# The entry of the FFN: the last ends of the sub-layer are recorded ahead of the ordinary products

## The chip, the cores and the metric

The kernel runs on one core of one Trainium2 chip. Its engines are TensorE (PE in the rows: matrix products and transposes), VectorE (DVE), ScalarE (ACT), GpSimd (POOL), and SyncE (SP), which issues most DMAs. The metric is the device time of one launch in microseconds.

## The reference, cut to what matters

One inference step of a decoder trunk of two layers, for 1024 prompt tokens and 32 sample tokens, all in float32. Layer 0 has a pooling and state-space mixer, layer 1 an attention. Each layer ends with an FFN between two norms, and it is the passage from the sub-layer into that FFN that is changed:

```python
hp = hp + rms_norm(y_p, g[1])
hp = hp + rms_norm(swiglu_ffn(rms_norm(hp, g[2]), ffn_w_gate[layer], ffn_w_up[layer], ffn_w_down[layer]), g[3])

def swiglu_ffn(x, w_gate, w_up, w_down):
    return (jax.nn.silu(x @ w_gate) * (x @ w_up)) @ w_down
```

`y_p` is the output projection of the mixer, `x @ w_out`, of 1024 columns; the hidden width of the FFN is 2816. The sample tokens take the same path (`hs`, `y_s`).

## The kernel before

**Numbers in two parts.** Every float32 operand of a product is split into a high part (`whi` for weights, cast on ScalarE) and a low part (`wlo`, a subtraction on GpSimd or VectorE). A product is then three matmuls, lines 171 to 173 (`mm3`): high by high, low by high, high by low.

**The tokens.** The 1056 tokens are kept in columns, in four quarters (0 to 3); the output projection (`proj_out`) makes quarters 0 and 2 first, then 1, then 3. Each quarter ends in tiles of 128 tokens: tiles 6 and 7 are those of quarter 3, and tile 8 holds the 32 sample tokens. Tiles 6, 8 and 7, in this order, are the last ends of the sub-layer.

**The end of a tile** (`Boundary`, driven by the three-stage pipeline `Tiles`) is this chain. Eight transposes turn the tile into token rows in a PSUM bank (`turn`, line 329, bank `tp`, of which there are two). ScalarE squares and sums it (line 207) and takes the root (line 209). VectorE takes the reciprocal (211), scales (338) and adds the residual (342); the residual's rows `h` are loaded by SP (line 419 or 411) into one of two buffers. The same norm is made once more of the sum (`stats2`), with the normed rows `xs` (line 353, one buffer), and eight transposes turn them back (`turn2`, line 360). `Blocks` then writes them, split in two parts, as the operand blocks of the FFN: for the first half of the tokens `left` alone (B11, B21: lines 265 and 266), for the second half also `right1`, `right2` and `right3` (lines 279 to 296), which make B22 and the sums T1 to T4 in a scratch buffer `tmp` that exists once.

**The FFN's products.** Gate and up products are made for chunks of 256 hidden columns. Each chunk uses seven block products instead of eight (`seven`, bank `pp`), with sums S1 to S4 of the weights (`Weights.split`, lines 1151 to 1165: casts on ScalarE, low parts on GpSimd, sums on VectorE). For chunk 0, the quarters 0 and 2 (pair 0) are multiplied by ordinary products (`plain`, bank `mm`, 96 matmuls for gate and 96 for up), which need only B11, B21, B12 and B22 of that pair; these are ready before the last three ends. The gate product goes through Silu into `ct` (line 1256), and the up product is multiplied into it (`put0`, line 1252) and stored to `hd`. Quarters 1 and 3 of chunk 0, and all of the other ten chunks, go through `seven`.

**What sets the order.** In this part no order is written out. The recorded instructions go to a scheduler, which keeps one list for each engine; among the instructions that are ready in its own model of time, the one recorded earlier goes first. `proj_out` is a generator: it yields `po, ct` before its last three tiles, and the loop over `poc` records them. Each engine then runs its list strictly in order. Weights come through two shared buffers `wraw`, which free up when ScalarE and GpSimd have read them; `raws(kind)` with a kind takes a buffer of the scope `xS` instead, here `xe`, which T4 of pair 1 uses later. S1 to S4 lie where B12 lay, so they wait for the last ordinary product that reads B12.

Of the kernel before, what the change touches and what calls it, by code (L numbers as in the profile page):

```python
# [12 lines left out]
AF = mybir.ActivationFunctionType  # L13
# [41 lines left out]
def dram_ap(base, offset, pattern):  # L55
    return bass.AP(tensor=base.tensor, offset=base.offset + offset, ap=[list(x) for x in pattern])
# [3 lines left out]
def step_kernel(ctx, tc, x_prompt, x_sample, state_pool, state_s5, cache_k, cache_v, norm_gains,  # L60
# [6 lines left out]
    V, A, G, T = nc.vector, nc.scalar, nc.gpsimd, nc.tensor  # L67
# [29 lines left out]
    def nm(s):  # L97
        uid[0] += 1
        return f"{s}_{uid[0]}"

    def mmbank():
        return banks[-1].pool.tile([P, 512], F32, name=nm("mm"), tag="mm", bufs=banks[-1].mm)
# [67 lines left out]
    def mm3(ps, wh, wl, xh, xl, start, stop):  # L170
        T.matmul(ps, wh, xh, start=start, stop=False)  # L171
        T.matmul(ps, wl, xh, start=False, stop=False)  # L172
        T.matmul(ps, wh, xl, start=False, stop=stop)  # L173
# [864 lines left out]
    for j in range(2):  # L1038
        pt = mmbank()
        T.transpose(pt[:, 0:P], h0[:, j * P:(j + 1) * P], ident)  # L1040
        o = s5.tile([P, 64, 2], F32, name=nm("s5o"), tag="ut", bufs=4)
# [10 lines left out]
    with tc.tile_pool(name="glu", bufs=2) as glu:  # L1052
        wg = [weights(dram_ap(w_glu, j * 256, [[512, P], [P * 512, 4], [1, 256]]), a=4) for j in range(2)]
        for y in yS.q:
# [4 lines left out]
            for m in range(4):  # L1059
                wh, wl = wg[m // 2]  # L1060
                ms = slice((m % 2) * P, (m % 2) * P + P)
                ps = mmbank()
# [65 lines left out]
    def ffn(layer, xS, Y, poc, after, side):  # L1128
# [88 lines left out]
        def raws(kind):  # L1217
            if kind:
                t = xS.pool.tile([P, 2, 4, 256], F32, name=nm("raw2"), tag=kind, bufs=1)
                return [t[:, h] for h in range(2)]  # L1220
            return [wraw().rearrange("p (k c) -> p k c", k=4) for _ in range(2)]
# [6 lines left out]
        def plain(w, kind, evac):  # L1228

            rs = raws(kind)  # L1230
            ws = []
            for j, raw in enumerate(rs):
                nc.sync.dma_start(raw, dram_ap(w, base + j * 512 * HID, [[HID, P], [P * HID, 4], [1, 256]]))
                hi, lo = (wpool.tile([P, 1024], F32R, name=nm(n), tag=n, bufs=4).rearrange("p (k i c) -> p k i c", k=4, i=2)
                          for n in ("whi", "wlo"))
                A.copy(hi, four(raw))
                G.tensor_tensor(lo, four(raw), hi.bitcast(F32), op=sub)
                ws.append((hi, lo))
            ps = [mmbank() for _ in range(2)]
            for j, names in ((1, ("B12", "B22")), (0, ("B11", "B21"))):  # L1240
                for i in range(2):
                    for half, name in enumerate(names):
                        bh, bl = blk[name, 0]
                        wh, wl = ws[half]
                        for k in range(4):
                            mm3(ps[i][:, j * 256:j * 256 + 256], wh[:, k, i], wl[:, k, i], bh[:, k], bl[:, k],
                                half == 0 and k == 0, half == 1 and k == 3)
            for i in range(2):
                evac(i, ps[i], ct[:, 4 * (w is w_up) + 2 * i:4 * (w is w_up) + 2 * i + 2].rearrange("p a b -> p (a b)"))
# [3 lines left out]
            for j in range(2):  # L1253
                nc.scalar.dma_start(hd[i][:, j * HALF:j * HALF + 256], o[:, j * 256:j * 256 + 256])

        plain(w_gate, None, lambda i, ps, o: A.activation(o, ps, AF.Silu))
        plain(w_up, "xe", put0)
        for _ in poc:
            pass
        po.close()  # L1260
        f = Scope(nm("ffn"), side)
        banks[-1].close()
# [77 lines left out]
    def after0():  # L1340
# [10 lines left out]
        return done  # L1351

    ffn(0, x1S, yS, poc, after0, "left")
    norm_scope.pop().close()
    x2S = nxt["x"]
# [37 lines left out]
    class Project:  # L1393
# [27 lines left out]
        def evac(self, n0, n, ps):  # L1421
            a, c = n0 // P, (min(n0 + n, SEQ) - n0) // P
            nat = lambda t: t[:, :SEQ].rearrange("p (c s) -> p s c", s=L)[:, a:a + c]
            src = ps[:, 0:c * P].rearrange("p (s c) -> p s c", s=c)
            if self.part == 0:
                A.activation(nat(self.hi), src, AF.Copy, scale=0.125)
                V.scalar_tensor_tensor(nat(self.lo), src, 0.125, nat(self.hi).bitcast(F32), op0=mult, op1=sub)
            else:
                A.copy(nat(self.ft), src)
            if n0 + n == NT:  # L1430
                rows = ps[:, c * P:n].rearrange("p (t b) -> p t b", t=TS)
                if self.part == 0:
                    A.activation(self.rows, ps[:, c * P:n], AF.Copy, scale=0.125)
                else:
                    A.copy(self.rows.rearrange("p (b t) -> p t b", t=TS), rows)
# [618 lines left out]
    def after1():  # L2054
# [10 lines left out]
        return done  # L2065

    ffn(1, x3S, y1S, poc, after1, "right")
    norm_scope.pop().close()
    banks[-1].close()
# [46 lines left out]
```

## Time and profile before

| | |
|---|---|
| median of 3 runs | 2817.33 us (2815.06 to 2820.85) |
| the profiled execution | 2814.3 us, of which 2812.5 us are its span |
| TensorE busy | 2624.1 us, 93% |
| VectorE, GpSimd, ScalarE busy | 1666.5 us, 1380.5 us, 1112.8 us |
| FFN entry of layer 0 | products up to 444.74 us, last ends up to 477.46 us |
| FFN entry of layer 1 | products up to 2054.45 us, last ends up to 2087.13 us |

Times in the rows count from the start of the span. A timeline row gives start and length in microseconds, engine, line, operation, out<-in by the program's names, shape and count; in brackets stands how long the engine was idle before it, and what ended that. Rows of matmuls follow each other more closely than their lengths, since they are pipelined. A row of stretches gives the length, for each engine the busy time with the number of instructions, then the clock that TensorE was granted, as a share of full speed, the share of the DMA engines, and GB/s.

### The profile page before, as it was taken

What the parts mean: (1) busy time and instruction counts of PE and PEld (TensorE: products, weight loads), DVE (VectorE), ACT (ScalarE), POOL (GpSimd) and SP (SyncE); (2) the same over time, 40 slices, a digit from 0 to 9 for tenths busy, and PEclk for the clock granted to TensorE, in tenths of its full rate; (3) what the DMA queues carried; (4) which work ended last, traced back from release to release, by engine and by line L of the source; (5) the groups of instructions that cost most, each with busy time, mean ns of one, the idle gap of its engine ahead of it and who ended that gap; (6) DMA issues with size and microseconds to landing.
All of it is one profiled execution on the core that took longest, in us unless ns stands there. A gap on an engine that the chain in (4) does not pass through costs nothing.

```text
span 2812.5 us, 49713 instructions
## 1 busy us (share of the span) xinstructions
PE 2624.1 (93%) x19556; PEld 2527.7 (90%) x19556; DVE 1666.5 (59%) x3027; ACT 1112.8 (40%) x2033; POOL 1380.5 (49%) x1004
## 2 busy tenths in 40 slices
PE   6598996999999999989999999999969999999998
PEld 6587996999999999989899777778969999999998
DVE  8778375655554355743343699993766555543555
ACT  4134464222222311333344688884642222233112
POOL 4954454454554644012554466674543545455440
PEclk9799997999999999999999999999979999999999
DMA  5253452222122422243887666654622222232223
GB/s 150 101 194 117 121 188 79 84 81 84 65 92 83 154 92 92 86 159 124 230 251 205 167 170 159 165 144 143 197 77 75 86 73 83 74 107 93 92 92 131
DMA packets 272397, 348.64 MB, mean 124 GB/s; under 512 B 43864, under 2 KB 204380, under 8 KB 272156
## 3 DMA queue, kind: packets, MB, share of 16 engines
q1 hardware_dynamic: 213140, 287.72, 34.2%
q10 hardware_dynamic: 57872, 53.55, 5.6%
q0 software_dynamic: 1152, 4.19, 0.4%
q8 instruction: 154, 2.52, 0.4%
q14 instruction: 79, 0.65, 0.1%
HBM read 266.19 MB, written 79.39 MB: 123 GB/s over the span
## 4 chain that ended last, share of the span: by engine, by line
PE 74%; DVE 10%; DMA 5%; issue 4%; ACT 3%; POOL 2%; SPq 1%; ACTq 0%; POOLq 0%; DVEq 0%
PE pp L172 10%; PE pp L171 10%; PE pp L173 10%; PE mm L171 7%; PE mm L173 7%; PE mm L172 7%; PE tp L173 2%; PE tp L171 2%; PE tp L172 2%; PE tq L171 2%; PE tq L172 2%; PE tq L173 2%; PE pt L1910 1%; DVE pl L1927 1%; DVE Pr L1886 1%
## 5 line engine op out<-in xcount | busy, mean ns | idle before, releaser
L171 PE MATMUL pp<-blk,whi 128*128 128x272 f32 (+1 forms) x2352 | 673.6, 288 | 16.4 <-ACT blk L295 10.9
L172 PE MATMUL pp<-blk,wlo 128*128 128x272 f32 (+1 forms) x2352 | 676.3, 289 | 0.9 <-POOL wlo L1152 0.8
L173 PE MATMUL pp<-blk,whi 128*128 128x272 f32 (+1 forms) x2352 | 673.2, 287 | 0.0
L142 POOL TENSOR_TENSOR wlo<-wraw,whi 128x1024 fp32r<-128x1024 f32 x102 | 246.1, 2422 | 563.6 <-ACT whi L141 512.5
L171 PEld LDWEIGHTS pp<-blk,whi 128*128 128x128 f32 x2352 | 450.2, 192 | 17.4 <-ACT blk L295 11.5
L172 PEld LDWEIGHTS pp<-blk,wlo 128*128 128x128 f32 x2352 | 449.8, 192 | 1.4 <-POOL wlo L1152 1.4
L173 PEld LDWEIGHTS pp<-blk,whi 128*128 128x128 f32 x2352 | 450.2, 192 | 0.0
L1183 DVE TENSOR_TENSOR c<-pp,c 128x528 f32<-128x528 f32 (+1 forms) x308 | 209.2, 680 | 357.1 <-PE pp L173 351.0
L1152 POOL TENSOR_TENSOR wlo<-S,whi 128x1024 fp32r<-128x1024 f32 x82 | 199.5, 2433 | 371.9 <-ACT whi L1151 371.7
L141 ACT CAST whi<-wraw 128x1024 fp32r<-128x1024 f32 x126 | 131.1, 1053 | 357.7 <-PE mm L173 105.1
L1151 ACT CAST whi<-S 128x1024 fp32r<-128x1024 f32 x88 | 92.4, 1050 | 356.4 <-PE pp L173 332.8
L173 PE MATMUL mm<-hid,whi 128*128 128x256 f32 (+1 forms) x680 | 194.4, 286 | 8.1 <-POOL hid L1291 8.1
L171 PE MATMUL mm<-hid,whi 128*128 128x256 f32 (+1 forms) x680 | 197.6, 291 | 1.8 <-DVE yacc L1312 1.8
L172 PE MATMUL mm<-hid,wlo 128*128 128x256 f32 (+1 forms) x680 | 194.4, 286 | 0.0
L171 PE MATMUL mm<-y,whi 128*128 128x256 f32 (+1 forms) x576 | 167.4, 291 | 1.7 <-DVE s5o L1042 1.3
L172 PE MATMUL mm<-y,wlo 128*128 128x256 f32 (+1 forms) x576 | 166.9, 290 | 0.0
L173 PE MATMUL mm<-y,whi 128*128 128x256 f32 (+1 forms) x576 | 166.9, 290 | 0.0
L1312 DVE TENSOR_TENSOR yacc<-mm,yacc 128x272 f32<-128x272 f32 (+1 forms) x264 | 113.2, 431 | 81.5 <-PE mm L173 81.4
L171 PE MATMUL tp<-hid,whi 128*128 128x272 f32 x484 | 138.3, 286 | 0.0
L172 PE MATMUL tp<-hid,wlo 128*128 128x272 f32 x484 | 138.0, 285 | 0.0
L173 PE MATMUL tp<-hid,whi 128*128 128x272 f32 x484 | 137.7, 285 | 0.0
L173 PEld LDWEIGHTS mm<-hid,whi 128*128 128x128 f32 x680 | 128.7, 190 | 8.9 <-POOL hid L1291 8.9
(532 smaller groups left out, 7432.5 us busy)
## 6 DMA issues: line engine op xcount, KB each, us to landing
raw<-in_ffn_w_up_dram SPq DMA_DIRECT2D x48, 512.0 KB
wraw<-in_ffn_w_gate_dram SPq DMA_DIRECT2D x48, 512.0 KB
hid<-hd SPq DMA_DIRECT2D x44, 528.0 KB
wraw<-in_ffn_w_down_dram SPq DMA_DIRECT2D x44, 512.0 KB
hd<-c ACTq DMA_DIRECT2D x80, 264.0 KB
wraw<-in_ab_w_out_dram SPq DMA_DIRECT2D x24, 512.0 KB
wraw<-in_c_w_qkv_dram ACTq DMA_DIRECT2D x24, 512.0 KB
kt<-in_cache_k_dram SPq DMA_DIRECT2D x32, 384.0 KB
```

Of the source, the lines that this page charges most:

```text
L141: A.copy(hi[:rows], raw[:rows])
L142: lo_eng.tensor_tensor(lo[:rows], raw[:rows], hi[:rows].bitcast(F32), op=sub)
L171: T.matmul(ps, wh, xh, start=start, stop=False)
L172: T.matmul(ps, wl, xh, start=False, stop=False)
L173: T.matmul(ps, wh, xl, start=False, stop=stop)
L1151: A.copy(hi, src)
L1152: (V if early and src is S34 else G).tensor_tensor(lo, src, hi.bitcast(F32), op=sub)
L1183: plus = lambda o, ps, x: V.tensor_tensor(o, ps, x, op=add)
L1312: V.tensor_tensor(yo, ps[:, :n], yo, op=add)
L1886: V.tensor_tensor_reduce(out=self.p[:, c0:c0 + n], in0=ps, in1=strip[:, off:off + n], scale=-1.0, scalar=self.mx if part else -NEG, op0=ad ...
L1910: T.transpose(pt[:, j, r * P:(r + 1) * P], self.u.rows[r].p[:, (self.j0 + j) * P:(self.j0 + j + 1) * P], ident)
L1927: V.tensor_tensor(self.pl[:, a, b], self.pt[:, a, b], self.ph[:, a, b].bitcast(F32), op=sub)
```

## The change

The loop that records the last three tiles' ends moves ahead of the two ordinary products, so the scheduler prefers the ends where both are ready. The up product's raw weights lose their own buffer, since T4 has `xe` by then, and come through the two `wraw` buffers.

```diff
--- before.py
+++ after.py
@@ -1253,10 +1253,10 @@
             for j in range(2):
                 nc.scalar.dma_start(hd[i][:, j * HALF:j * HALF + 256], o[:, j * 256:j * 256 + 256])
 
-        plain(w_gate, None, lambda i, ps, o: A.activation(o, ps, AF.Silu))
-        plain(w_up, "xe", put0)
         for _ in poc:
             pass
+        plain(w_gate, None, lambda i, ps, o: A.activation(o, ps, AF.Silu))
+        plain(w_up, None, put0)
         po.close()
         f = Scope(nm("ffn"), side)
         banks[-1].close()
```

Each instruction of the ends, of the products and of chunk 0's weights is there before and after, apart from table loads of ScalarE. Their places in the lists differ, in both layers alike; beyond the entries only a few neighbours have changed places. Numbers in the names count the program's tiles and differ between the two programs.

**TensorE, layer 0, end of the ordinary products, before.** `mm_4565` is the second half of the up product, `tp` are the turns of tiles 6, 8 and 7 (from `yo`) and their second transposes (from `xs`), `pp` is the first block product:

```order
L171 MATMUL mm_4565<-blk_3715,whi_4560 128x256
L172 MATMUL mm_4565<-blk_3715,wlo_4561 128x256
L173 MATMUL mm_4565<-blk_3715,whi_4560 128x256
L329 MATMUL tp_4668<-ident,yo_4183 128x128 x8
L329 MATMUL tp_4686<-ident,yo_3843 32x128 x8
L329 MATMUL tp_4719<-ident,yo_4183 128x128 x8
L360 MATMUL tp_4730<-ident,xs_4717 128x128 x8
L360 MATMUL tp_4780<-ident,xs_4767 128x32 x8
L360 MATMUL tp_4821<-ident,xs_4811 128x128 x8
L171 MATMUL pp_4916<-blk_4160,whi_4863 128x272
```

**TensorE now, in the middle of the gate product.** `tp_4172` is the second transposes of tile 3, `mm_4634` the first half of the gate product, `tp_4441` the turn of tile 6:

```order
L360 MATMUL tp_4172<-ident,xs_4170 128x128 x8
L172 MATMUL mm_4634<-blk_3715,wlo_4626 128x256
L173 MATMUL mm_4634<-blk_3715,whi_4625 128x256
L171 MATMUL mm_4634<-blk_3715,whi_4625 128x256
L329 MATMUL tp_4441<-ident,yo_4183 128x128 x8
```

**TensorE now, end of the up product** (`mm_4747`):

```order
L171 MATMUL mm_4747<-blk_3715,whi_4742 128x256
L172 MATMUL mm_4747<-blk_3715,wlo_4743 128x256
L173 MATMUL mm_4747<-blk_3715,whi_4742 128x256
L360 MATMUL tp_4553<-ident,xs_4540 128x32 x8
L360 MATMUL tp_4594<-ident,xs_4584 128x128 x8
L171 MATMUL pp_4917<-blk_4160,whi_4864 128x272
```

The turn of tile 6 stands behind 55 of the 192 product matmuls, that of tile 8 behind 86, that of tile 7 behind 106, and the second transposes of tile 6 behind 151. Only the second transposes of tiles 8 and 7 are left behind the last product.

**ScalarE, layer 0, before.** `tp_4172` is tile 3, `tp_4668` tile 6, `tp_4686` tile 8, `mm_4453` and `mm_4454` the gate product, `whi` the first chunk's weights:

```order
L265 CAST blk_4160<-tp_4172 128x2x4x128
L1256 ACT_TABLE_LOAD
L1256 ACTIVATE ct_3166<-mm_4453 128x512
L1151 CAST whi_4863<-wraw_4857 128x4x128
L1256 ACTIVATE ct_3166<-mm_4454 128x512
L1151 CAST whi_4869<-S_800_4861 128x1024
L1254 DMA hd_4440<-ct_3166 128x256 x2
L1151 CAST whi_4873<-wraw_4858 128x1024
L1151 CAST whi_4879<-S_801_4862 128x1024
L1254 DMA hd_4440<-ct_3166 128x256 x2
L207 ACTIVATE junk_4679,ss_4680<-tp_4668 128x1024
L209 ACT_TABLE_LOAD
```

**ScalarE now, from tile 3 on.** `tp_4441` and `h_4450` are tile 6, `tp_4459` is tile 8, `mm_4634` and `mm_4635` the gate product:

```order
L209 ACTIVATE sd_4455<-ss_4453,epst 128x1
L1258 ACT_TABLE_LOAD
L1258 ACTIVATE ct_3166<-mm_4634 128x512
L1151 CAST whi_4864<-wraw_4858 128x4x128
L207 ACTIVATE junk_4473,ss_4474<-tp_4459 32x1024
L209 ACT_TABLE_LOAD
L209 ACTIVATE sd_4476<-ss_4474,epst 32x1
L207 ACTIVATE junk_4483,ss_4484<-h_4450 128x1024
L1258 ACT_TABLE_LOAD
L1258 ACTIVATE ct_3166<-mm_4635 128x512
L209 ACT_TABLE_LOAD
L209 ACTIVATE sd_4486<-ss_4484,epst 128x1
```

The squares and roots of tiles 6 and 8 stand between the two Silus and around them, and the table is loaded four times in each entry instead of twice. The three casts of 1024 columns of chunk 0's weights have moved behind tile 8's second root.

**VectorE, layer 0, before, behind the blocks of tile 3.** `S` are the sums of chunk 0's gate weights, `ct` the products with the Silu, `wlo` the low part of S3 and S4, `tp_4668` and `h_4677` tile 6, `tp_4686` and `h_4695` tile 8:

```order
L1158 TENSOR_TENSOR S_800_4861<-wraw_4857,wraw_4858 128x4x128
L1164 TENSOR_TENSOR S_801_4862<-wraw_4857 128x4x128
L1159 TENSOR_TENSOR S_800_4861<-S_800_4861,wraw_4857 128x4x128
L1165 TENSOR_TENSOR S_801_4862<-wraw_4858,S_800_4861 128x4x128
L1252 TENSOR_TENSOR ct_3166<-mm_4564,ct_3166 128x512
L1252 TENSOR_TENSOR ct_3166<-mm_4565,ct_3166 128x512
L1152 TENSOR_TENSOR wlo_4880<-S_801_4862,whi_4879 128x1024
L211 RECIPROCAL rs_4684<-sd_4682 128x1
L338 SCALAR_TENSOR_TENSOR tp_4668<-tp_4668,rs_4684,g_543_3159 128x1024
L211 RECIPROCAL rs_4705<-sd_4703 32x1
L342 TENSOR_TENSOR h_4677<-h_4677,tp_4668 128x1024
L338 SCALAR_TENSOR_TENSOR tp_4686<-tp_4686,rs_4705,g_543_3159 32x1024
```

**VectorE now, from tile 7's scaling on.** `tp_4492` and `h_4501` are tile 7, `xs_4540` is tile 8, `tmp_4522` and `blk_4526` are tile 6's blocks:

```order
L338 SCALAR_TENSOR_TENSOR tp_4492<-tp_4492,rs_4517,g_543_3159 128x1024
L1158 TENSOR_TENSOR S_801_4862<-wraw_4858,wraw_4859 128x4x128
L1164 TENSOR_TENSOR S_802_4863<-wraw_4858 128x4x128
L1159 TENSOR_TENSOR S_801_4862<-S_801_4862,wraw_4858 128x4x128
L342 TENSOR_TENSOR h_4501<-h_4501,tp_4492 128x1024
L353 SCALAR_TENSOR_TENSOR xs_4540<-h_4468,rs_4535,g_544_3161 32x1024
L1165 TENSOR_TENSOR S_802_4863<-wraw_4859,S_801_4862 128x4x128
L283 TENSOR_TENSOR tmp_4522<-tp_4503,tmp_4522 128x512
L284 TENSOR_TENSOR blk_4526<-tp_4503,blk_4526 128x4x128
L1252 TENSOR_TENSOR ct_3166<-mm_4746,ct_3166 128x512
L211 RECIPROCAL rs_4579<-sd_4577 128x1
L1252 TENSOR_TENSOR ct_3166<-mm_4747,ct_3166 128x512
```

The four sums and the products with the Silu (and three rows further on the low part of S3 and S4) stood ahead of the ends and now stand among them: between tile 7's scaling and tile 6's last block.

## Rows read from the trace of the kernel before

**Rows 1.** The page, part 1: TensorE busy, its share of the span, instructions.

```profile
PE 2624.1 (93%) x19556; PEld 2527.7 (90%) x19556; DVE 1666.5 (59%) x3027; ACT 1112.8 (40%) x2033; POOL 1380.5 (49%) x1004
```

**Rows 2.** Stretches: length, engines busy (instructions), granted clock, DMA share; two FFN entries.

```profile
core 0: us, PE busy (x) PEld busy (x) DVE busy (x) ACT busy (x) POOL busy (x), PEclk, DMA share, GB/s
428.10:444.74 16.64, 16.64 (x142) 16.64 (x141) 4.50 (x6) 6.11 (x7) 4.37 (x3) 1.00 0.15 48
437.62:448.37 10.75, 9.03 (x77) 8.66 (x75) 6.26 (x7) 4.90 (x6) 4.77 (x2) 1.00 0.31 98
444.74:477.46 32.72, 11.48 (x63) 9.98 (x61) 25.64 (x34) 18.49 (x39) 14.26 (x14) 0.57 0.22 76
456.17:468.61 12.44, 3.99 (x21) 3.52 (x22) 11.00 (x13) 5.83 (x13) 4.16 (x3) 0.50 0.24 84
468.61:477.46 8.85, 3.61 (x18) 3.29 (x16) 5.12 (x11) 4.23 (x11) 7.73 (x10) 0.50 0.00 1
2054.45:2087.13 32.68, 11.01 (x62) 9.60 (x60) 25.65 (x34) 18.51 (x39) 14.24 (x14) 0.64 0.22 76
```

**Rows 3.** Timeline of TensorE: start, length, line, tiles, count [idle before, releaser].

```profile
427.07 1.03 PE L360 MATMUL tp<-ident,xs 128*128 128x128 f32 x8
...
444.74 1.91 PE L329 MATMUL tp<-ident,yo 128*128 128x128 f32 x16
...
452.31 1.94 PE L329 MATMUL tp<-ident,yo 128*128 128x128 f32 x8 [5.66 <-DVE h L342]
...
467.56 1.94 PE L360 MATMUL tp<-ident,xs 128*128 128x128 f32 x8 [5.62 <-DVE xs L353]
...
477.46 0.60 PE L171 MATMUL pp<-blk,whi 128*128 128x272 f32 x1 [5.24 <-ACT blk L295]
```

**Rows 4.** Timeline of ScalarE, layer 0: Silu, casts, square, its sum, table load, root.

```profile
430.53 0.60 ACT L1256 ACTIVATE ct<-mm 128x512 f32<-128x512 f32 x1
...
432.02 0.62 ACT L1151 CAST whi<-wraw 128x512 fp32r<-128x512 f32 x1 [0.89 <-PE mm L173]
...
439.60 1.05 ACT L1151 CAST whi<-S 128x1024 fp32r<-128x1024 f32 x1 [5.59 <-DVE S L1159]
...
446.59 1.02 ACT L207 ACTIVATE junk<-tp 128x1024 bf16<-128x1024 f32 x1 [0.56 <-issue]
...
447.51 0.19 ACT L207 ACTIVATION_READ_ACCUMULATOR junk<-tp 128x1 f32 x1
...
447.73 1.28 ACT L209 ACT_TABLE_LOAD   x1
...
449.02 0.29 ACT L209 ACTIVATE sd<-ss,epst 128x1 f32<-128x1 f32 x1
```

**Rows 5.** Chain of work, layer 0: start, length, what.

```profile
456.06 3.38 DMA h<-in_x_prompt_dram
```

**Rows 6.** Timeline of VectorE, layer 0.

```profile
417.88 2.82 DVE L353 SCALAR_TENSOR_TENSOR xs<-h,rs,g 128x1024 f32<-128x1024 f32 x1
...
437.62 0.69 DVE L1158 TENSOR_TENSOR S<-wraw,wraw 128x512 f32<-128x512 f32 x1 [7.20 <-PE mm L172]
...
454.71 1.28 DVE L353 SCALAR_TENSOR_TENSOR xs<-h,rs,g 128x1024 f32<-128x1024 f32 x1
...
467.33 1.28 DVE L296 TENSOR_TENSOR blk<-tmp,blk 128x512 fp32r<-128x512 f32 x2
...
491.24 2.87 DVE L1158 TENSOR_TENSOR S<-wraw,wraw 128x512 f32<-128x512 f32 x1 [1.39 <-POOL wlo L1152]
```

**Rows 7.** Timeline of GpSimd, layer 0.

```profile
417.25 2.37 POOL L1237 TENSOR_TENSOR wlo<-wraw,whi 128x1024 fp32r<-128x1024 f32 x1 [4.48 <-ACT whi L1236]
...
440.72 2.40 POOL L1152 TENSOR_TENSOR wlo<-S,whi 128x1024 fp32r<-128x1024 f32 x1 [6.72 <-ACT whi L1151]
```

**Rows 8.** Timeline of SP's queue, layer 0.

```profile
421.19 0.39 SPq L1140 DMA_DIRECT2D wraw<-in_ffn_w_gate_dram  x1
...
479.87 0.94 SPq L1140 DMA_DIRECT2D raw<-in_ffn_w_up_dram  x2
```

## The prediction

> **What bounds the kernel now.** I read the page first: TensorE is busy for 93% of the span [rows 1], so a change of order can gain only where TensorE stands still. Then I cut the entry of each FFN into stretches [rows 2]. In the 16.64 us from 428.10 us the ordinary products run without a gap at full clock. In the next 32.72 us TensorE is busy for 11.48 us, at 0.57 of its clock, while VectorE is busy for 25.64 us. Layer 1 shows the same stretch: 32.68 us, of which 11.01 us are busy. So the second stretch is what can be filled, and the first is what could fill it.
>
> TensorE's timeline says what the second stretch waits for [rows 3]; the end of a row names the idle time before it and what ended it. At 444.74 us the products have ended, and the transposes of tiles 6 and 8 (first "turn") run together. Tile 7's turn waits 5.66 us, its second transposes, at 467.56 us, another 5.62 us, and the first product that needs T1 or T2 of the last tile waits 5.24 us, to 477.46 us. These transposes take 1.94 us at half the clock, where those of 427.07 us took 1.03 us. It is one chain through ScalarE (squares, square roots), VectorE (scaling, residuals, differences of blocks) and the load of tile 7's residual row block. Its last piece hangs on the single buffer `tmp`: after tile 6's last block is written, at 467.33 + 1.28 = 468.61 us [rows 6], tile 8's small blocks and then tile 7's follow, and 8.85 us later [rows 2] the T blocks are there.
>
> **What the change removes, adds and moves.** Of the 192 product matmuls, 55 now stand ahead of tile 6's turn on TensorE and 137 behind it (before: all 192 ahead). One matmul takes 0.12 us (16.64 us for the 142 instructions of the first stretch [rows 2]). The turn now starts three matmuls after the second transposes of 427.07 us [rows 3], at which 52 products were done, so at about 428.2 us instead of 444.74 us (0.8 us for the eight transposes, three times 0.12 us). The head start is 16.5 us, and the 137 matmuls are now cover for the chain. The question is how much of the 16.5 us is left at the end of the chain. I walk it in the clock of the profiled execution.
>
> *ScalarE.* Its queue is in order, and the changed order puts both Silus between the square roots. From 429.2 us, when the turn ends, stand: tile 6's square (1.02 us and 0.19 us for its sum), its root (0.29 us), a table load (1.28 us), the first Silu (0.60 us), one cast of 512 columns of a weight (0.62 us), then tile 8's square [rows 4]. Tile 8's turn comes 31 matmuls after tile 6's, 3.7 us, and takes 1.0 us, so that square begins at 434.0 us, 0.8 us after ScalarE is free for it. Behind it: load, root, tile 6's second square, load, second Silu, load, root, by the same rows: 1.2 + 1.28 + 0.29 + 1.2 + 1.28 + 0.60 + 1.28 + 0.29 = 7.4 us, less some 0.6 us by which neighbours overlap: 440.8 us. Before, only one load, at 447.73 us, stood in this chain [rows 4]; the first was under the products. Tile 6's normed rows (`xs`, a reciprocal and 1.28 us [rows 6]) are ready at 442.3 us; before it was 455.99 us. So 13.7 us of the head start are left here.
>
> *The load of tile 7's rows* waits for that, as before, and takes 3.38 us [rows 5]: 445.8 us. *ScalarE goes on* with two squares and roots, to 443.8 us, and VectorE can scale tile 7 from 443.9 us.
>
> *VectorE.* From that scaling to tile 6's last block VectorE had 13 instructions, 11.00 us busy, before [rows 2]. In the changed order seven more stand among them: the four sums and differences of the first chunk's gate weights (S1 to S4), the two products with the Silus, and the low part of S3/S4. Before, these seven ran under the matmuls, for 6.26 us between 437.62 and 448.37 us [rows 2]. They lose their cover: 11.00 + 6.26 = 17.3 us, so 461.2 us. Tile 7's residual comes after three of the seven, at 447.2 us, later than its load, which therefore hides.
>
> *Collisions with GpSimd.* The low parts of S1/S2 and of the second half of the gate weights, 1024 columns each, 2.40 us on GpSimd [rows 7], ran under the products or beside the first turn. Now they start when S1/S2 exist, inside that VectorE queue. What a meeting costs is in the trace: `xs` took 2.82 us at 417.88 us, beside a GpSimd operation that began at 417.25 us, against 1.28 us alone [rows 6, 7]. Two meetings at 1.54 us are 3.1 us: 464.3 us. Lower bound: none, 0 us. Upper bound: a sum of weights that met GpSimd took 2.87 us [rows 6], against 0.69 us alone, so 2.2 us a meeting and four meetings, 8.7 us. I take the two, for two operations were moved in.
>
> The Trainium skill, "SBUF — State Buffer", section "Who interferes with whom", says that a VectorE instruction with two SBUF inputs and a GpSimd instruction that reads SBUF exclude each other for a whole instruction. By that the two meetings would cost at most 2 x 2.40 = 4.8 us instead of 3.1 us; the row of 2.82 us is within it.
>
> *The rest* of the chain, tile 8's and tile 7's blocks, is not touched: 464.3 + 8.85 = 473.1 us instead of 477.46 us. That is 4.4 us for layer 0. TensorE's work is the same and its order behind this point too, and the next gate, the load of the first chunk's up weights into `tmp`, at 479.87 us [rows 8], waits for the same blocks and moves with them. Layer 1 has the same order and the same two stretches, so 4.4 us again.
>
> *The weights.* The up weights of the products no longer have a buffer of their own (`xe`), and go through the two shared `wraw` buffers. On SP's queue they take the places at which the first chunk's gate halves were loaded, the second of them at 421.19 us [rows 8]; these go one turn back. The second of them waits for GpSimd's last low part of the products, about 430.5 us (load issued at 421.19 us; 3.38 us by an equally large load [rows 5], with a margin of 2 us; a cast of 1.05 us [rows 4]; 2.4 us), and lands about 435 us. VectorE asks for it at 445.2 us. The cover is 10 us, so I cost this at nothing. Were it gone, tile 7's residual, queued behind that sum, would lose one for one.
>
> **Sum.** 2 x 4.4 = 8.8 us. The profiled execution took 2814.3 us for a span of 2812.5 us, so 2805.5 us against its own time; the median of the runs is 3.0 us above it, 2817.33 us, which gives 2808.5 us.
>
> **The rivals.**
> - *The chain moves as one block.* Then each layer gains the 16.5 us, and the time is 2784 us. For it: 21.2 us of TensorE's stretch are idle [rows 2]. Against it: the seven VectorE instructions and the extra table loads stand inside the chain now.
> - *The gain is eaten.* Four meetings instead of two, at 1.54 us, or as much lost in waits of ScalarE around the table loads, leave 7.4 - 6.2 = 1.2 us a layer: 2815 us. For it: VectorE is busy for 25.64 us of the 32.72 us already, and gets work added [rows 2]. Against it: with no meeting at all the gain is 477.46 - 461.2 - 8.85 = 7.4 us, so 4.6 us have to be lost before the gain is under 0.2%. The Trainium skill, "ScalarE: Activation LUTs", section "What ACT_TABLE_LOAD costs", gives 1.38 us of draining beside the 1.28 us of a load. Here the root starts at 449.02 us, when the load of 447.73 us has just ended [rows 4]; by the page's figure three more loads would take 4.1 us a layer and leave 0.3 us, so 2816.7 us, which is an estimate from that page.
> - *Slower.* VectorE meets GpSimd at five or more of its instructions in this queue, at 2.2 us each: 10.9 us against the 7.4 us there are, 3.5 us a layer lost, 2824 us. It decides from the fourth meeting. For it: GpSimd's two operations on weights and its three on tile 6's blocks lie in the stretch, and many of VectorE's instructions there work on SBUF alone, as the one of 2.87 us does [rows 6]. Against it: all five would have to fall on such an instruction, at its dearest.
> - *The change does nothing* is excluded by the order itself: the turns did move.
>
> **How the numbers follow.** Forecast 0.72, block 0.06, eaten 0.17, slower 0.05. A difference under about 0.2%, 5.6 us, can't be told from none with these runs. Three meetings at 1.54 us leave 2.8 us a layer, 5.6 us, and none leave 14.8 us; that is the forecast's own range, 2802.5 to 2811.7 us. Faster: 0.71 of the forecast's 0.72 and the block, 0.77. Same: 0.18. Slower: 0.05. For 8 times in 10 the range takes in most of the eaten case above and a part of the way to the block below: 2799 to 2815 us.
>
> **What would show it.** Right: tile 6's turn within a microsecond of the end of the transposes before it, about 16 us ahead of the end of the products; four table loads in each entry instead of two; the product that needs T1 or T2 starting 4 to 5 us earlier than 477.46 us in layer 0 and 2087.13 us in layer 1; TensorE idle mainly after the products, with VectorE running without a pause from tile 7's scaling to tile 6's last block; `xs` or the block sums over 2 us where GpSimd works on weights. Wrong: a first chunk that starts 8 us or more earlier (no meetings), or VectorE waiting for the second gate half, or a shift at the entry that the FFN behind it does not keep.

## The result, and the profile after

The changed kernel took 2806.7 us (median of 7 runs, 2800.7 to 2810.9) beside 2821.5 us of the kernel before (7 runs, 2815.1 to 2826.7): a ratio of 0.9949, 95% interval [0.9933, 0.9965], which makes 14.4 us less. Two more measurements of the same kernel, with other runs of before, gave 0.9979 [0.9965, 0.9992] and 0.9974 [0.9959, 0.9988]. Weighted by the inverse squares of their intervals the three make 0.9969 [0.9961, 0.9977], 8.7 us less; the first one is the extreme, and it differs from the second by more than their intervals allow, so the interval of the three together is too narrow. The medians of the changed kernel agree (2806.7, 2809.0 and 2807.8 us); it was before that lay high beside the first one, with 2821.5 us against 2816.8 and 2814.6 us beside the others. The forecast was 8.8 us.

The profiled execution of the first measurement took 2810.5 us (span 2808.7 us), only 3.8 us less than that of before. The page says no more than that TensorE is busy for as long as before [rows 1]:

```profile
PE 2627.7 (94%) x19556; PEld 2529.9 (90%) x19556; DVE 1674.2 (60%) x3027; ACT 1118.1 (40%) x2037; POOL 1387.4 (49%) x1004
```

The stretches say where it went. The first row is the part of the products from tile 6's turn on, the second goes from their end to the first product that needs T1 or T2, the third from tile 7's scaling to tile 6's last block, the fourth is the rest of the chain, the last is layer 1's second (compare [rows 2]):

```profile
core 0: us, PE busy (x) PEld busy (x) DVE busy (x) ACT busy (x) POOL busy (x), PEclk, DMA share, GB/s
434.45:455.02 20.57, 20.26 (x171) 19.78 (x169) 12.99 (x17) 17.28 (x27) 5.56 (x5) 1.00 0.29 87
455.02:478.64 23.62, 5.71 (x29) 4.99 (x29) 19.82 (x24) 9.61 (x21) 17.97 (x15) 0.58 0.26 86
450.18:469.82 19.64, 9.84 (x67) 9.23 (x66) 19.55 (x20) 8.05 (x13) 10.79 (x5) 0.72 0.41 131
469.82:478.64 8.82, 0.71 (x5) 0.39 (x3) 5.10 (x10) 4.23 (x11) 7.72 (x10) 0.50 0.00 1
2058.28:2081.91 23.63, 5.71 (x30) 4.99 (x29) 19.82 (x24) 9.62 (x21) 17.97 (x15) 0.61 0.26 87
```

The stretch behind the products is 23.6 us instead of 32.7 us; the products themselves became longer by the turns they now hold. From tile 7's scaling on VectorE is busy for 19.55 of 19.64 us: it is the bound there. TensorE's timeline, to be read against [rows 3], in which the same turns start at 444.74 and 452.31 us:

```profile
433.22 1.04 PE L360 MATMUL tp<-ident,xs 128*128 128x128 f32 x8
434.45 1.03 PE L329 MATMUL tp<-ident,yo 128*128 128x128 f32 x8
439.03 1.03 PE L329 MATMUL tp<-ident,yo 128*32 128x128 f32 x8
...
449.04 1.06 PE L360 MATMUL tp<-ident,xs 128*128 128x128 f32 x8 [0.31 <-DVE rs L211]
...
463.88 1.94 PE L360 MATMUL tp<-ident,xs 128*128 128x128 f32 x8 [7.57 <-DVE xs L353]
...
478.64 0.60 PE L171 MATMUL pp<-blk,whi 128*128 128x272 f32 x1 [8.11 <-ACT blk L295]
```

The absolute times can't be compared: this execution reached tile 2's second transposes at 425.83 us, that of before at 420.85 us, though TensorE's and VectorE's instructions up to there stand in the same order. What can be compared is the interval from the start of tile 3's second transposes (427.07 us before, 433.22 us after) to the product that needs T1 or T2. It went from 50.39 to 45.42 us in layer 0 and from 50.35 to 45.43 us in layer 1: 4.9 to 5.0 us a layer, 9.9 us in all. All experiments below are read by this interval:

| kernel | tile 2's second transposes, layer 0 | interval, layer 0 / 1 (us) | from there to the 472nd TensorE instruction behind, layer 0 / 1 (us) | ratio to before |
|---|---|---|---|---|
| before | 420.85 | 50.39 / 50.35 | 65.9 / 65.9 | 1 |
| changed | 425.83 | 45.42 / 45.43 | 64.3 / 67.0 | 0.9949 |
| changed, second time | 420.06 | 45.68 / 45.43 | 66.0 / 66.1 | 0.9979 |
| changed, third time | 420.81 | 45.44 / 45.43 | 65.9 / 65.4 | 0.9974 |
| up weights alone | 426.12 | 50.58 / 50.42 | 64.3 / 66.1 | 0.9997 [0.9985, 1.001] |
| order alone | 424.45 | 45.42 / 45.44 | 66.1 / 64.5 | 0.9967 [0.9952, 0.9982] |
| copy for Silu | 422.74 | 40.55 / 41.82 | 64.3 / 65.8 | 0.9945 [0.9927, 0.9964] |
| no low parts | 426.18 | 41.44 / 42.41 | 67.0 / 65.8 | 0.9945 [0.9926, 0.9964] |
| late gate | 424.44 | 41.57 / 41.88 | 64.3 / 65.8 | 0.993 [0.9906, 0.9954] |
| late gate, second time | 424.69 | 41.49 / 41.60 | 65.6 / 65.8 | 0.9946 [0.9928, 0.9965] |
| early sums | 419.24 | 46.64 / 45.37 | 65.6 / 67.1 | 0.9959 [0.994, 0.9978] |
| both | 424.62 | 44.72 / 42.62 | 65.7 / 66.0 | 0.9971 [0.9953, 0.9988] |
| low parts on VectorE | 420.56 | 40.48 / 40.44 | 65.9 / 66.2 | 0.9934 [0.9916, 0.9952] |

In the two changed kernels that were measured more than once (changed and late gate) the interval repeats within 0.4 us; in four of the others the two layers differ by 1.0 to 2.1 us. The second and fourth columns scatter more: up to 7 us are won or lost ahead of the entry, and up to 2.8 us in the 472 instructions behind it, whichever kernel runs. So one pair of profiles can show 3.8 us where the two entries gain 9.9 us.

ScalarE has four table loads in the entry where it had two (compare [rows 4]); between tile 6's two roots, at 436.67 and 447.08 us, it pauses for 0.6 us of 10.4 us:

```profile
436.67 0.29 ACT L209 ACTIVATE sd<-ss,epst 128x1 f32<-128x1 f32 x1
436.98 1.28 ACT L1258 ACT_TABLE_LOAD   x1
...
441.23 1.28 ACT L209 ACT_TABLE_LOAD   x1
...
443.87 1.28 ACT L1258 ACT_TABLE_LOAD   x1
445.17 0.60 ACT L1258 ACTIVATE ct<-mm 128x512 f32<-128x512 f32 x1
445.79 1.28 ACT L209 ACT_TABLE_LOAD   x1
447.08 0.30 ACT L209 ACTIVATE sd<-ss,epst 128x1 f32<-128x1 f32 x1
```

VectorE's queue, where the sums met GpSimd (compare [rows 6]): the last sum takes 2.83 us and tile 7's `xs` 3.02 us, L289 and the low part of S3/S4 are as long as before, and the sums wait for no weights:

```profile
450.18 1.29 DVE L338 SCALAR_TENSOR_TENSOR tp<-tp,rs,g 128x1024 f32<-128x1024 f32 x1
451.38 0.68 DVE L1158 TENSOR_TENSOR S<-wraw,wraw 128x512 f32<-128x512 f32 x1
...
453.18 1.21 DVE L342 TENSOR_TENSOR h<-h,tp 128x1024 f32<-128x1024 f32 x1
...
455.51 2.83 DVE L1165 TENSOR_TENSOR S<-wraw,S 128x512 f32<-128x512 f32 x1
...
460.73 3.02 DVE L353 SCALAR_TENSOR_TENSOR xs<-h,rs,g 128x1024 f32<-128x1024 f32 x1
463.66 1.76 DVE L289 TENSOR_TENSOR tmp<-tmp 128x512 f32<-128x512 f32 x1
465.34 2.29 DVE L1152 TENSOR_TENSOR wlo<-S,whi 128x1024 fp32r<-128x1024 f32 x1
...
467.76 0.68 DVE L290 TENSOR_TENSOR tmp<-tmp 128x512 f32<-128x512 f32 x1
```

GpSimd's low parts lie exactly there (compare [rows 7]), and its two last steps on tile 6's blocks behind them:

```profile
454.48 3.32 POOL L1152 TENSOR_TENSOR wlo<-S,whi 128x1024 fp32r<-128x1024 f32 x1 [13.46 <-ACT whi L1151]
...
460.31 2.35 POOL L1152 TENSOR_TENSOR wlo<-wraw,whi 128x1024 fp32r<-128x1024 f32 x1
462.61 3.94 POOL L296 TENSOR_TENSOR blk<-tmp,blk 128x512 fp32r<-128x512 f32 x2
```

### The profile page after: what moved, and what is told of

Read it like the earlier page. It is cut to its first block, busy times and chain, and to the rows that moved or that the text cites. A ratio compares the mean times of both kernels' runs of the same rounds, so it can differ in the third digit from the quotient of the medians.

```text
span 2808.7 us, 49710 instructions
## 1 busy us (share of the span) xinstructions
PE 2627.7 (94%) x19556; PEld 2529.9 (90%) x19556; DVE 1674.2 (60%) x3027; ACT 1118.1 (40%) x2037; POOL 1387.4 (49%) x1004
## 4 chain that ended last, share of the span: by engine, by line
PE 71%; DVE 12%; issue 5%; DMA 5%; ACT 4%; POOL 2%; SPq 1%; ACTq 0%; POOLq 0%; DVEq 0%
PE pp L172 10%; PE pp L171 10%; PE pp L173 10%; PE mm L171 6%; PE mm L173 6%; PE mm L172 6%; PE tp L173 2%; PE tp L172 2%; PE tp L171 2%; PE tq L171 2%; PE tq L172 2%; PE tq L173 2%; PE pt L1910 1%; DVE pl L1927 1%; DVE Pr L1886 1%
```

## The experiments

In the kernels of the experiments the line numbers are up to 13 higher than in the changed kernel; the names out<-in tell which instruction a row shows.

**The changed kernel again** (twice, unchanged).

> The changed kernel once more, unchanged, beside the same runs of the kernel before as the other three. Theory (only the two entries gain): in the trace the product that needs T1 or T2 starts 45.4 us behind the start of tile 3's second transposes in each layer, as in the first trace of the changed kernel, against 50.4 us before; that is 5.0 us a layer, 10 us in all, a ratio of 0.9965. Rival (something outside of the entries gains too, for instance the up weights that are no longer loaded early): 14 us or more, a ratio of 0.995 or less, and the two traces differ elsewhere by a constant 4 to 5 us that comes back in this run.

> The changed kernel a third time, beside the late-gate kernel. Theory: 45.4 us in both layers again and 9.9 us less than before, 0.9965. Rival: a ratio of 0.995 or less as in the first measurement, so that something outside of the entries gains.

Measured: 0.9979 and 0.9974; the interval is 45.68 / 45.43 and 45.44 / 45.43 us. Nothing outside of the entries comes back in all three: ahead of the entry the three start at 425.83, 420.06 and 420.81 us. So the 4 to 5 us by which the first ratio exceeds the entries do not belong to the change; they lie in the high runs of before.

**The up weights alone**, in the kernel before:

```diff
-        plain(w_up, "xe", put0)
+        plain(w_up, None, put0)
```

> The kernel before with one line of the change: the up weights of the ordinary product go through the two shared buffers, the order of the ends and the products stays. Theory: these weights cost and bring nothing: the product that needs T1 or T2 starts 50.4 us behind tile 3's second transposes, as before, and the time is within 0.1% of before. Rival: the 4 to 5 us by which the first measured difference (14 us) exceeds the two entries come from here: 0.9983 of before, 4 to 5 us less, with the 50.4 us unchanged. Second rival: the second chunk-0 gate half now comes late under the products: 1 to 3 us slower.

Measured: 0.9997 [0.9985, 1.001], interval 50.58 / 50.42 us. In the order of before the weights cost and bring nothing that can be seen here.

**The order alone.** The weights of both products are loaded and split ahead of the ends, the products stay behind them:

```diff
+        eg, eu = early(w_gate, None), early(w_up, "xe")
         for _ in poc:
             pass
-        plain(w_gate, None, lambda i, ps, o: A.activation(o, ps, AF.Silu))
-        plain(w_up, None, put0)
+        plain(w_gate, eg, lambda i, ps, o: A.activation(o, ps, AF.Silu))
+        plain(w_up, eu, put0)
```

> The change of order alone: the ends are recorded ahead of the ordinary products, but the weights of these products are loaded and split ahead of the ends, the up weights early and in the buffer xe as before. Theory: as the changed kernel: 45.4 us from tile 3's second transposes to the product that needs T1 or T2, time within 0.1% of the changed kernel. Rival (the weights bring 4 to 5 us of their own): 4 to 5 us slower than the changed kernel at the same 45.4 us. Second rival (weights through the shared buffers cost something, hidden in the sum): the 45.4 us shrink by 1 us or more.

Measured: 0.9967 [0.9952, 0.9982], interval 45.42 / 45.44 us. The whole gain is the order's.

**No table switches.**

```diff
-        plain(w_gate, None, lambda i, ps, o: A.activation(o, ps, AF.Silu))
+        plain(w_gate, None, lambda i, ps, o: A.copy(o, ps))
```

> The changed kernel with a copy in place of the Silu of the ordinary gate product (this leaves the Silu of that product out), so that ScalarE loads no table between the square roots of the ends; the order on every engine is otherwise that of the changed kernel. Theory: three of the table loads, 3 x 1.28 = 3.84 us, stand in the chain of tiles 6 and 8 and delay everything behind; without them xs of tile 6, tile 7's row load and VectorE's queue start 3.8 us earlier, and the product that needs T1 or T2 starts 41.6 us behind tile 3's second transposes instead of 45.4 us; 7.7 us less than the changed kernel in all. Rival (the chain waits for tile 8's and 7's turns behind the products, or VectorE's products with the gate wait for the end of the up product, so that the loads are hidden): under 1 us a layer. Second rival (a switch drains more than its 1.28 us): over 5 us a layer.

Measured: 0.9945 [0.9927, 0.9964], interval 40.55 / 41.82 us. In layer 1 that is 3.61 us less than the changed kernel, 1.20 us for each of the three loads; at tile 7's scaling, ahead of VectorE's queue, it is 3.90 us (13.08 instead of 16.98 us behind tile 3's second transposes). TensorE there (tile 3's second transposes stood at 2025.31 us):

```profile
2052.36 1.94 PE L360 MATMUL tp<-ident,xs 128*128 128x128 f32 x8 [5.14 <-DVE xs L353]
...
2067.13 0.59 PE L171 MATMUL pp<-blk,whi 128*128 128x272 f32 x1 [8.12 <-ACT blk L295]
```

So three of the four loads stand in the chain in full, and they cost about their own length. The Trainium skill, "ScalarE: Activation LUTs", section "What ACT_TABLE_LOAD costs", gives some 1.38 us of draining beside each load; by that figure three would have brought an estimated 8 us, and this run does not agree. Layer 0 gained 1.3 us more than layer 1 from the same order of instructions: there the last sum took 0.67 us and tile 7's `xs` 1.75 us instead of 2.90 and 3.01 us, while L289 and L290 took 2.84 and 1.56 us instead of 1.75 and 0.68 us.

**No low parts beside VectorE.** The low parts of S1/S2 and of the second half are not made (the high parts stand in for them):

```diff
                     A.copy(hi, src)
+                    if self.first and two and src is not S34:
+                        return hi, hi
```

> The changed kernel without the two GpSimd low parts of the first gate chunk that fall into VectorE's queue (S1/S2 and the second half: their high parts are taken in place of the low parts, which leaves this part of the computation out). Theory: GpSimd's work beside it is what makes two VectorE instructions long (the last sum, 2.83 us, and the normed rows xs of tile 7, 3.02 us, where such instructions take 0.69 and 1.28 us alone); without it both are short again and the product that needs T1 or T2 starts 3.9 us earlier, 41.5 us behind tile 3's second transposes instead of 45.4 us; 7.8 us less in all. Rival (these lengths have another cause, or the lost time is given back in a wait for GpSimd's three own steps on tile 6's blocks): less than 1.5 us a layer. Rival (the meetings only move to other VectorE instructions of the queue, since GpSimd's steps on the blocks come earlier): about 2 us a layer.

Measured: 0.9945 [0.9926, 0.9964], interval 41.44 / 42.41 us, 3.98 and 3.02 us less than the changed kernel. VectorE in layer 1: the last sum is short, tile 7's `xs` has lost 1.08 of its 3.02 us, and the low part of S3/S4 takes 1.21 us where the changed kernel's took 2.29 us:

```profile
2056.72 0.67 DVE L1167 TENSOR_TENSOR S<-wraw,S 128x512 f32<-128x512 f32 x1
...
2059.77 1.94 DVE L353 SCALAR_TENSOR_TENSOR xs<-h,rs,g 128x1024 f32<-128x1024 f32 x1
...
2063.32 1.21 DVE L1154 TENSOR_TENSOR wlo<-S,whi 128x1024 fp32r<-128x1024 f32 x1
```

Added up that is 2.16 + 1.08 + 1.08 = 4.3 us off the queue; 1.3 us of it are lost again further up, where tile 6's second transposes stood 17.1 us behind tile 3's instead of 15.8 us. The trace shows what was late there: on ScalarE the cast of the up product's second weights half stands ahead of tile 3's blocks and of tile 6's square, and it waited for its load until 2.56 us behind the start of tile 3's second transposes (2033.14 us), against 0.17 us in the changed kernel's layer 1:

```profile
2035.70 1.05 ACT L1238 CAST whi<-wraw 128x1024 fp32r<-128x1024 f32 x1 [5.18 <-DMA wraw<-in_ffn_w_up_dram]
```

**The gate late.** Both Silus wait for tile 7's second root, by a bias that is a zero made from that root:

```diff
+        z = zero()
+        A.activation(z, last_sd[0], AF.Copy, scale=0.0)
-        plain(w_gate, None, lambda i, ps, o: A.activation(o, ps, AF.Silu))
+        plain(w_gate, None, lambda i, ps, o: A.activation(o, ps, AF.Silu, bias=z))
```

> The changed kernel with both Silus of the ordinary gate product held back until ScalarE has taken tile 7's second root (their bias is a zero made from that root; nothing is left out). One table load is then left in the ends, and none in the first chunk behind them. Theory: the three loads that stood in the chain are gone as in the run with a copy for the Silu, so 41.6 us from tile 3's second transposes to the product that needs T1 or T2 in layer 1, and 40.6 us in layer 0; 7 to 10 us less than the changed kernel. Rival: the products with the gate, on VectorE, now wait for the late Silus (root, zero, cast, load, Silu: 3.5 us behind the root) and everything queued behind them is late: 2 us or more of the gain are given back, 43.5 us or more.

> The kernel with the late Silus once more, beside the changed kernel under the same runs of before, to size it: it had few undisturbed runs the first time. Theory: 3.7 us a layer less than the changed kernel in the entries (41.7 against 45.4 us) makes 7.4 us, a ratio to the changed kernel of 0.9974, and to before of 0.9938. Rival: the first ratio of 0.993 was luck, and only the 1.28 us load that vanishes from the first chunk counts: 2 us less than the changed kernel.

Measured: 0.993 [0.9906, 0.9954] and 0.9946 [0.9928, 0.9965], together some 17 us less than before; intervals 41.5 to 41.9 us. In layer 0 of the first one 40.6 us had been expected, as in the copy run, but the last sum met GpSimd there (2.89 us). Beside the third measurement of the changed kernel the median is 2798.8 us against 2807.8 us. One load is left in the entry and none behind it, and VectorE waits 0.48 us for the gate in layer 0 and 0.18 us in layer 1. ScalarE in layer 1 (L211 is the root, L1265 the Silu):

```profile
2051.49 0.29 ACT L211 ACTIVATE sd<-ss,epst 128x1 f32<-128x1 f32 x1
2051.81 0.20 ACT L1264 ACTIVATE zero<-sd 128x1 f32<-128x1 f32 x1
2052.26 1.05 ACT L1154 CAST whi<-wraw 128x1024 fp32r<-128x1024 f32 x1 [0.25 <-PE mm L173]
2053.33 1.28 ACT L1265 ACT_TABLE_LOAD   x1
2054.63 1.26 ACT L1265 ACTIVATE ct<-mm,zero 128x512 f32<-128x512 f32 x2
```

**The sums early.** S1 to S4 of chunk 0's gate go into `xe`, and are recorded ahead of the last stages of the ends:

```diff
+                if self.first:
+                    S = xS.pool.tile([P, 2, 4, 2, P], F32, name=nm("S"), tag="xe", bufs=1)
+                    S12, S34 = S[:, 0], S[:, 1]
...
+            if q == 3:
+                yield
             tiles.flush()
...
-        for _ in poc:
-            pass
+        next(poc)
...
+        g0 = split(w_gate, 0, None)
+        for _ in poc:
+            pass
```

> The changed kernel with the four sums of the first gate chunk in the buffer xe, which is free there, instead of the place of B12: they no longer wait for the last product that reads B12 and are recorded ahead of the last tiles' rest. Theory: their 4.9 us on VectorE (three of 0.69 us and one of 2.83 us) leave the queue between tile 7's scaling and tile 6's last block and run in VectorE's idle time before it; about 1 us is given back because tile 6's scaling now stands behind a sum that waits for the second gate half. 41.4 us instead of 45.4 us to the product that needs T1 or T2, 8 us less in all. Rival (VectorE's queue isn't what sets the end; the load of tile 7's rows or ScalarE's queue takes over at once): under 1.5 us a layer. Rival (the wait for the second gate half costs more than it saves): slower than the changed kernel.

Measured: 0.9959 [0.994, 0.9978], interval 46.64 / 45.37 us: no gain over the changed kernel, and this theory was wrong. The queue from tile 7's scaling to tile 6's last block did shrink, from 19.64 to 17.13 us in layer 0. But the sums stand ahead of tile 6's scaling now, and two of them wait for the gate weights; tile 6's `xs` then ends 20.5 us behind tile 3's second transposes (444.49 - 423.98) instead of 15.7 us (448.89 - 433.22), where I had allowed 1 us; in layer 1 it is 19.1 us. Tile 7's row load starts as much later, and its residual waits for it, 2.25 us in layer 1 (the last row; the first two are of layer 0):

```profile
427.65 2.15 DVE L1170 TENSOR_TENSOR S<-wraw 128x512 f32<-128x512 f32 x1 [4.10 <-DMA wraw<-in_ffn_w_gate_dram]
...
433.31 0.69 DVE L1164 TENSOR_TENSOR S<-wraw,wraw 128x512 f32<-128x512 f32 x1 [2.31 <-DMA wraw<-in_ffn_w_gate_dram]
...
2052.50 1.22 DVE L342 TENSOR_TENSOR h<-h,tp 128x1024 f32<-128x1024 f32 x1 [2.25 <-DMA h<-hB]
```

**Both together.** Here the Silus and the products with the gate are also recorded behind the ends, so the run is not the sum of the two edits alone.

> Late Silus and early sums together. If both terms were independent, 45.4 - 3.8 - 4.0 = 37.6 us to the product that needs T1 or T2. Theory: less than that sum, because VectorE's products with the gate can't come before the end of the up product, 21.8 us behind tile 3's second transposes; from there some 8 us of VectorE's queue and the 8.8 us of tile 8's and 7's blocks follow: 39.3 us, 6 us a layer and 12 us in all less than the changed kernel. Rival (independent): 37.6 us, 15 us less in all. Rival (one cause counted twice, as both only empty the same queue ahead of tile 7): no better than the better of the two alone, 41 us.

Measured: 0.9971 [0.9953, 0.9988], interval 44.72 / 42.62 us, an interval longer than with the late gate alone and than in all three expectations: the early sums again delay tile 6, and with it tile 7's root, for which the late Silus wait, so that VectorE now waits 2.02 us for the gate as well:

```profile
457.62 0.69 DVE L1265 TENSOR_TENSOR ct<-mm,ct 128x512 f32<-128x512 f32 x1 [2.02 <-ACT ct L1271]
```

**The low parts on VectorE**, on top of the late gate:

```diff
-                    (V if early and src is S34 else G).tensor_tensor(lo, src, hi.bitcast(F32), op=sub)
+                    (V if early and (src is S34 or self.first and two) else G).tensor_tensor(lo, src, hi.bitcast(F32), op=sub)
```

> The late-gate kernel, with the two low parts of the first gate chunk that met VectorE (S1/S2 and the second half) computed on VectorE itself instead of on GpSimd. Theory: GpSimd's 2.4 us cost VectorE 2.2 us each when they meet; VectorE does the same subtraction in 1.2 us alone. Its queue gets 2 x 1.2 = 2.4 us longer and loses 2.2 + 2.1 us (last sum and xs of tile 7 as in the late-gate trace, 2.90 and 3.35 us against 0.69 and 1.28 us): 2 us less a layer, 39.8 us from tile 3's second transposes to the product that needs T1 or T2 instead of 41.7 us; 4 us less in all than the late-gate kernel. Rival: the meetings go on with GpSimd's own steps on tile 6's blocks (the low parts then take 2.3 us, as the low part of S3/S4 does in the changed kernel): no gain, or up to 1 us a layer slower than the late-gate kernel.

Measured: 0.9934 [0.9916, 0.9952], interval 40.48 / 40.44 us: 1.0 to 1.4 us a layer less than the late gate, between theory (2 us) and rival. The last sum (0.67 us) and tile 7's `xs` (1.26 us) are short. But now GpSimd waits: its two steps on tile 6's blocks took 3.94 us in the changed kernel (from 462.61 us) and take 6.97 us, and VectorE's own last blocks take 3.25 us instead of 1.46 us:

```profile
449.44 6.97 POOL L299 TENSOR_TENSOR blk<-tmp,blk 128x512 fp32r<-128x512 f32 x2 [2.88 <-ACT blk L298]
```

```profile
449.97 1.26 DVE L356 SCALAR_TENSOR_TENSOR xs<-h,rs,g 128x1024 f32<-128x1024 f32 x1
...
453.70 3.25 DVE L299 TENSOR_TENSOR blk<-tmp,blk 128x512 fp32r<-128x512 f32 x2
```

By median (2795.2 us of 6 runs) this is the fastest kernel of the study; its ratio can't be told from the late gate's.

## Why the prediction was right, point by point

All times from the start of tile 3's second transposes, in layer 0.

| step | predicted | measured |
|---|---|---|
| tile 6's turn | 1.1 | 1.2 |
| tile 8's square | 6.9 | 6.9 |
| tile 6's `xs` ready | 15.2 | 15.7 |
| tile 7's scaling | 16.8 | 17.0 |
| tile 7's residual | 20.1 | 20.0 |
| tile 6's last block | 37.2 | 36.6 |
| product that needs T1 or T2 | 46.0 | 45.4 |

- *The head start.* As predicted, all three turns and tile 6's second transposes run under the products.
- *ScalarE.* Right, and the experiment with the copy shows its price: 3.6 us a layer of the head start went into three loads.
- *The loads of rows and weights hide.* Right in this execution: no wait stands before the sums at 451.38 us or the residual at 453.18 us, and the run with the up weights alone is as fast as before. One term was overlooked: the up weights are not cast early any more, and in the changed order ScalarE's cast of their second half stands ahead of tile 6's square. In this execution it starts 1.1 us before the start of tile 3's second transposes in layer 0, in others up to 2.6 us behind it (no low parts, layer 1). Where it was 1.5 us late in the changed kernel itself (second time, layer 0) the interval is 0.25 us longer than in layer 1; in the order-alone run, where these weights are split ahead of the ends, tile 6's second transposes stand 15.8 us behind tile 3's in both layers.
- *VectorE's queue.* Predicted 17.3 us of work and 3.1 us of meetings, measured 19.64 us. Two meetings was the right count of those that the change brought, at another price: 2.14 us for the sum, 1.74 us for `xs`, 3.9 us together instead of 3.1 us. What I had overlooked is that the 17.3 us already held three meetings of before, each about 1 us above the 0.68 and 1.21 us that such instructions take alone:

```profile
446.07 2.29 DVE L1152 TENSOR_TENSOR wlo<-S,whi 128x1024 fp32r<-128x1024 f32 x1 [0.37 <-ACT whi L1151]
...
462.85 1.69 DVE L289 TENSOR_TENSOR tmp<-tmp 128x512 f32<-128x512 f32 x1
...
464.58 1.64 DVE L290 TENSOR_TENSOR tmp<-tmp 128x512 f32<-128x512 f32 x1
```

Of these, L290 is short now (0.68 us), and L289 and the low part have stayed long (1.76 and 2.29 us), the low part beside another operation of GpSimd than before. The balance is 2.9 us, so that the forecast's 3.1 us came close by luck. That would make 20.2 us; that it is less fits with instructions that follow without a pause, which start some 0.08 us ahead of the end of the one before (450.18 + 1.29 = 451.47 us, next start 451.38 us), and there are more of these now. The run without the low parts shows that the new meetings are GpSimd's: 3.0 to 4.0 us a layer.

- *The rest of the chain.* 8.82 us instead of 8.85 us: not touched, as predicted.
- *The sum.* 4.4 us a layer predicted, 4.9 to 5.0 us measured in the interval; 8.8 us predicted in all, 8.7 us (6.5 to 11.0 us) by the three measurements together. That 8.8 and 8.7 agree so closely is luck: the three measurements lie between 5.9 and 14.4 us, and the two entries gain 9.9 us in the traces. The median of 2806.7 us lies 1.8 us under the forecast; as the ratios differ from each other by more than that, this is not evidence of a further term. The sign that I had given for it, a start earlier than 477.46 us, fails as it was put: in layer 0 the product starts at 478.64 us, because this execution reached the entry late. Only the interval shows the gain.
- *The rivals.* The chain did not move as one block (that would be an interval of 33.9 us). The gain was not eaten, though most of the head start was: of its 16.5 us, 13.2 us were left at tile 6's `xs` (15.7 us instead of 455.99 - 427.07 = 28.9 us [rows 3, 6]), and 5.0 us at the end. Of the 8.2 us between, 7.2 us went into VectorE's queue (19.64 instead of 12.44 us), and 1.1 us into tile 7's scaling, which now waits for ScalarE's roots for 1.3 us behind `xs` and did so for 0.2 us before. The slower case did not come, though VectorE met GpSimd at four instructions of this queue: two of the four were in the 17.3 us already.

What stays open is why executions differ ahead of the entry, and which of VectorE's instructions meet GpSimd in an execution: the copy run had the long last sum in layer 1 and not in layer 0, from the same order.

## What to carry to other kernels

Filling a wait by moving a chain ahead of independent work pays only in as far as the engines of the chain are not also fed by that work: here 16.5 us of head start on TensorE became 4.9 us, because the products' Silus brought table loads between the roots, and the sums of chunk 0's gate weights, which wait for the last product that reads B12, came into VectorE's queue. So after such a move look at what the filler puts between the chain's instructions on each in-order engine, and push that behind the chain by a dependency; that was worth nearly as much again (another 8 us). Before a piece of work is moved forward into idle time, ask what it waits for: the early sums brought the wait for their weights into the chain and lost all that they had saved.

## What the runs showed of the hardware that was not expected

- The 472 TensorE instructions behind the product that needs T1 or T2 took from 64.3 to 67.1 us. TensorE waits 2.7 us in them for VectorE (line 1183, which adds up block products), and in one execution it comes back at half the clock, 1.2 GHz, in another at 2.4 GHz. Before, layer 0, the wait and what follows it:

```profile
494.54:497.27 2.73, 0.01 (x2) 0.01 (x1) 2.67 (x2) 0.30 (x1) 2.73 (x2) 0.94 0.89 298
497.27:500.00 2.73, 2.73 (x12) 2.73 (x13) 0.44 (x1) 0.75 (x1) 2.63 (x2) 0.50 0.27 86
```

The same two stretches after the change:

```profile
495.50:498.21 2.71, 0.00 (x0) 0.00 (x0) 2.66 (x2) 0.29 (x1) 2.71 (x2) 1.00 0.90 269
498.21:501.00 2.79, 2.79 (x22) 2.79 (x23) 1.41 (x3) 0.76 (x1) 2.69 (x2) 1.00 0.37 120
```

- The waiting between VectorE and GpSimd goes both ways. A VectorE `xs` of 1.28 us took up to 3.35 us beside GpSimd (late gate, layer 1), and GpSimd's two subtractions for tile 6 took 6.97 us beside a VectorE that ran without a pause (low parts on VectorE, layer 0), against 2.94 us in the kernel before:

```profile
462.73 2.94 POOL L296 TENSOR_TENSOR blk<-tmp,blk 128x512 fp32r<-128x512 f32 x2
```

The Trainium skill, "SBUF — State Buffer", section "Who interferes with whom", says that a VectorE instruction with two SBUF inputs contends with a GpSimd instruction that reads SBUF. These rows agree. The `xs` of 3.35 us lost 2.07 us, less than one GpSimd operation of 2.40 us [rows 7]; the first of the two subtractions took 5.28 us, beside several VectorE instructions in a row of which none took more than 1.56 us, so GpSimd was kept out for longer than one of them.
